# Layer 0's attention joins: statistics stored at an earlier step, merge factors at a later one, two rope turns and the copies of probabilities put at other steps, the last head replanned

## The chip, the cores and the metric

The kernel runs on one core of a Trainium2 chip. The metric is the device time of one execution in microseconds (us); lower is better. A core has five engines that run side by side, each taking its own instructions strictly in order: TensorE (PE in the profile; its weight loads are shown as PEld), VectorE (DVE), ScalarE (ACT), GpSimd (POOL) and SyncE (SP). SP computes nothing here; it issues almost all of the DMAs, also in order. Engines wait for each other through semaphores only.

## The reference

A decoder trunk of two layers over 1024 tokens of width 1024. Layer 0 mixes tokens by dilated softmax attention, layer 1 by gated linear attention; a squared-ReLU MLP follows each. The change touches layer 0's attention only:

```python
DILATED_GROUPS = ((128, 1), (512, 4), (2048, 16))
def dilated_attention(h, w_in, w_out):
    qkv = (h @ w_in).reshape(B, S, N_GROUPS, 3, ATTN_HEADS, HEAD_DIM)
    for g, (window, dil) in enumerate(DILATED_GROUPS):
        q = apply_rope(qkv[:, :, g, 0], cos, sin) * (HEAD_DIM ** -0.5)
        k = apply_rope(qkv[:, :, g, 1], cos, sin)
        v = qkv[:, :, g, 2]
        o_g, lse_g = dilated_group_attention(q, k, v, dil, window // dil)
    alpha = softmax(stack(lses), axis=0)
    o = sum(alpha[..., None] * stack(outs))
    return o.reshape(B, S, ATTN_WIDTH) @ w_out
```

There are 8 heads of 128 channels and, per head, three groups with dilations 1, 4 and 16. Each group has its own queries, keys and values. A query row's three softmax results are weighted by their denominators (the "merge factors") and added.

## The kernel before

All large products are split into three matmuls of float32 halves (high and low parts) and use a seven-product scheme for 2 by 2 blocks. Values of all heads are computed first and kept in DRAM (`vscr`). Then the 24 **passes** p = 3h + g of `Heads` run, one per head h and group g. A pass computes one group's queries and keys of one head with 14 half products (7 slots of `SLOTS`, two halves each, six matmuls of 128x512 per half), and after each half `advance()` moves a counter, the **clock**, one step on. So pass p covers clocks c = 14p to c + 14, and everything else is hung between the half products by the clock: `at(t, fn, rank)` puts a function on clock t, and functions of one clock are issued in order of rank (5 if not given). This order is the program order of every engine's queue.

What hangs on the clock of a pass that starts at c:

- `keep` (ACT, line 1475, rank 0): copies of the product banks ("e1" at c+3, "e5" at c+7, "e2" at c+9, "e3" at c+13). "e5" must be out before the slot that starts after clock c+8 adds to the same bank V again; "e2" before the slot that starts after c+10 adds to X.
- `column` (DVE, line 1438, rank 1) at c+5, c+11, c+13 and c+15: makes half a query or key block; SP then copies its two partition halves crosswise (`cw`, lines 1439 and 1440). The function `turn` inside it (DVE, lines 1447 to 1455, rank 6) applies the rope with that copy, four clocks later.
- `load` (SP, line 1430) at c+3 fetches the next pass's weights in four DMAs of 256 KB, and `stage` cuts them into halves (ACT line 791, DVE lines 792 to 829).
- `follow` hangs the previous pass's attention on this one: `scores` (PE), `soft` (DVE and ACT: bias, minimum, exponential with sums; the numbers kept are the group's statistics), and `send`, which stores the statistics in DRAM (SP). For the first two groups this is `Attention`, for the third `Classes`. Each has scores at c+8 on; `Classes` has all its scores at c+8.
- `Join` merges head h-1 during the passes of head h; its clocks count from c = 14 * 3h. `begin` (SP, lines 1344 to 1348) loads the statistics of all three groups, `factors` (DVE and one ACT, lines 1358 to 1364) makes the merge factors, `spread` scales the stored probabilities by them (the third group on DVE, line 1311, the others block by block on ACT, line 1239), `turn` and `turn_classes` transpose probabilities on PE (lines 1262, 1318), `values` and `values_classes` copy the transposes out of PSUM on ACT (lines 1398, 1385) and multiply with the values on PE (lines 1271, 1326), `keep_classes` copies the third group's result (ACT, line 1392), and `join` adds (DVE, line 1405).

Seven heads are joined in this way. The eighth is joined in `tail`, during the output projection `out_proj`: there each block of 12 matmuls (`tick`) moves the clock two steps on. `W.pump` at the end of a tick loads and cuts projection weights (SP line 133, ACT line 152, DVE line 153); from the seventh block of the first half of the projection on it may run ahead by four loads. `drain_to` runs the rest of the clock up to the first half of the last join, and the second half of the projection goes on with the clock.

Tiles come from pools of fixed numbers of buffers (`t2`: 8 of 2 KB per partition, `k4`: 25 of 4 KB), banks of PSUM from a pool of 8.

Of the kernel before, what the change touches and what calls it, by code (L numbers as in the profile page):

```python
# [9 lines left out]
F32 = mybir.dt.float32  # L10
# [3 lines left out]
AF = mybir.ActivationFunctionType  # L14
# [5 lines left out]
P = 128  # L20
# [4 lines left out]
HEADS = 8  # L25
# [16 lines left out]
def hybrid_trunk(ctx, tc, x, norm_mix, norm_mlp, norm_fin, a_in, a_out, g_in, g_up, g_b, g_nw,  # L42
# [16 lines left out]
    def t2(shape, dt, name):  # L59
        return wk.tile(shape, dt, name=name, tag="t2", bufs=8)  # L60
# [14 lines left out]
    steps = deque()  # L75
# [186 lines left out]
    class Split:  # L262
# [4 lines left out]
        @staticmethod  # L267
        def at(tiles, k):
            n = 4 // len(tiles)
            return tiles[k // n][:, k % n, :]  # L270
# [489 lines left out]
    class Up:  # L760
# [96 lines left out]
        def copy(self, p, name):  # L857
            e = t2([P, 512], F32, name)
            act.activation(e, self.st[p]["X"], AF.Copy)  # L859
            self.st[p][name] = e  # L860
# [293 lines left out]
    clock = [0]  # L1154
# [36 lines left out]
    class Attention:  # L1191
# [74 lines left out]
        def values(self, half, po, t):  # L1266
            at_ = 0
            for i, (k, c, where) in enumerate(self.pieces(half)):
                n = 128 * len(c)
                o = po[:, where:where + n] if self.g == 0 else po.rearrange("p (m r) -> p r m", r=4)[:, where, :]  # L1270
                pe.matmul(o, self.v[:, k, :], t[:, at_:at_ + n], start=self.g == 0 and i == 0, stop=True,  # L1271
                          skip_group_check=True)
                at_ += n
# [5 lines left out]
            at(c + send, self.send)  # L1279

    class Classes(Attention):
        SOFT = 9, 10, 11, 12
        SEND = 13

        def scores(self, j):
            if j:
# [45 lines left out]
    class Join:  # L1332
# [48 lines left out]
            self.ps = self.g[2].turn()  # L1381

        def values_classes(self):
            t = t2([P, 512], F32, "pt")
            act.activation(t, self.ps, AF.Copy)
            self.po = self.g[2].values(t)

        def keep_classes(self):
            self.k = k4([P, S], F32, "oc")
# [1 line left out]
            for q in range(2):  # L1391
                act.activation(to[:, q], self.po[q].rearrange("p (i e m) -> p i e m", i=4, e=2), AF.Copy)

        def values(self, g, half):
            banks = self.banks.pop((g, half))
            t = (t2 if len(banks) == 1 else k4)([P, 512 * len(banks)], F32, "pt")
            for i, (ps, n) in enumerate(banks):
                act.activation(t[:, 512 * i:512 * i + n], ps[:, :n], AF.Copy)
            if g == 0:
                self.sum = bank("pO")  # L1400
            self.g[g].values(half, self.sum, t)
# [10 lines left out]
    class Heads(Up):  # L1412
# [20 lines left out]
        def column(self, p, b, half, bank_, e):  # L1433

            h, g = divmod(p, NG)
            c = t2([P, 512], F32, "c")
            w = t2([P, 512], F32, "cw")
            dve.tensor_tensor(c, bank_, e, op=OP.add)  # L1438
            sp.dma_start(w[0:64, :], c[64:128, :])
            sp.dma_start(w[64:128, :], c[0:64, :])  # L1440

            def turn():
                sl = slice(512 * half, 512 * half + 512)
                if (p, b) not in self.dst:
                    self.dst[p, b] = k4([P, S], F32, ("qT", "kT")[b])
                dst = self.dst[p, b]
                dve.tensor_tensor(w, w, ctab[:, 1, sl], op=OP.mult)  # L1447
                dve.tensor_tensor(c, c, ctab[:, 0, sl], op=OP.mult)
                if g == 0:
                    dve.tensor_tensor(dst[:, sl], c, w, op=OP.add)  # L1450
                else:
                    r = 4 if g == 1 else 16
                    n = 512 // r
                    o = dst.rearrange("p (r m) -> p r m", r=r)[:, :, n * half:n * half + n]
                    dve.tensor_tensor(o, c.rearrange("p (m r) -> p r m", r=r),
                                       w.rearrange("p (m r) -> p r m", r=r), op=OP.add)
            at(clock[0] + (3 if p == self.count - 1 and half else 4), turn, 6)

        def remain(self, fn):
            if self.behind:  # L1460
# [6 lines left out]
        def plan(self, p):  # L1467
            c = 14 * p
            st = self.st.setdefault(p, {})
            self.behind = True  # L1470

            def keep(b, name):
                def fn():
                    e = t2([P, 512], F32, name)
                    act.activation(e, st[b], AF.Copy)  # L1475
                    st[name] = e
                return fn
            at(c + 3, keep("X", "e1"), 0)
            at(c + 5, lambda: self.column(p, 0, 0, st["Y"], st["e1"]), 1)
            at(c + 7, keep("V", "e5"), 0)  # L1480
            at(c + 9, keep("X", "e2"), 0)
            at(c + 11, lambda: self.column(p, 1, 0, st["V"], st["e2"]), 1)
            at(c + 13, keep("X", "e3"), 0)
            at(c + 13, lambda: self.column(p, 1, 1, st["X"], st["e5"]), 1)
            at(c + 15, lambda: self.column(p, 0, 1, st["Z"], st["e3"]), 1)
            if p == 0:
                for s, t in ((4, 1), (6, 3), (5, 5)):
                    at(c + t, lambda s=s: self.stage(p, s), 7)
            at(c + 3, lambda: self.load(p + 1))
            for s, t in ((0, 8), (1, 9), (2, 10), (3, 11), (4, 14), (6, 15), (5, 17)):  # L1490
                at(c + t, lambda s=s: self.stage(p + 1, s), 1.5 if s in (1, 3, 6) else 7)

# [46 lines left out]
        keep_head(h, half, o)  # L1539
        reached.add((0, half))  # L1540

    def join_steps(load, first, gap=1):

        n = lambda k: first + int(gap * k)
        return ((load, 5, "begin"),
                (n(0), 9, "factors"), (n(0), 9.1, "spread", 2, None),
                (n(1), 5, "load_values", 2), (n(1), 9, "spread", 0, range(4)), (n(3), 5, "load_values", 0),
                (n(3), 9, "spread", 0, range(4, 8)), (n(4), 5, "load_values", 1),
                (n(4), 3, "turn_classes"), (n(4), 9, "spread", 1, range(0, 8, 2)),
                (n(5), 4, "values_classes"), (n(5), 9, "spread", 1, range(1, 8, 2)),  # L1550
                (n(6), 0.5, "keep_classes"), (n(6), 3, "turn", 0, 0),
                (n(7), 0.6, "values", 0, 0), (n(7), 3, "turn", 1, 0),
                (n(8), 0.6, "values", 1, 0), (n(8), 3, "turn", 0, 1),
                (n(9), 0.6, "values", 0, 1), (n(9), 0.5, "join", 0), (n(9), 3, "turn", 1, 1),
                (n(10), 0.6, "values", 1, 1),
                (n(11), 0.6, "join", 1))


    vals = RawValues(a_in, [(3 * g + 2) * AW for g in range(NG)], lambda g: vscr[:, g, :])
# [235 lines left out]
    for p in range(heads.count):  # L1795
        h, g = divmod(p, NG)
        if g == 0 and h:
            Join(h - 1, joined).plan(14 * p, join_steps(15, 19))
        if p == heads.count - 1:
            for k in range(0, KT, 2):  # L1800
                add_rows(a_out, k)
            c = 14 * p
            at(c + 1, lambda: turned.load(0), 0)
            at(c + 3, lambda: (W.dma(), W.dma()), 0)
            at(c + 4, lambda: (W.dma(), W.dma()), 0)
            for t in (7,8,9,10):
                at(c + t, lambda: W.prep(dve), 7)
            at(c + 8, lambda: turned.turn(0), 7)
            at(c + 9, lambda: (turned.load_x(0), turned.load_x(1)))
            at(c + 11, lambda: turned.turn(1), 7)  # L1810
        heads.run_head(p)

    def drain_to(mark):
        while mark not in reached:
            steps.popleft()()
            now[0] += 1
            run_due()

    def tail():

        c = clock[0]
        heads.follow(heads.count - 1, c, (7, 7, 8, 8), (8, 8, 9, 9), 10)
        turned.load(1)
        Join(HEADS - 1, last_joined).plan(c, join_steps(13, 18, 1.5))
        rows = {}

        def early(half):
            t = rows[half] = h8([P, 4, 512], F32, "ol2")
            sp.dma_start(t[:, 0:3, :], oscr[4:7, :, 512 * half:512 * half + 512].rearrange("h p c -> p h c"))

        def turn(half, h):
            keep_head(h, half, rows[half][:, h - 4, :])

        def weights():
            W.early = RAW
        at(c + 1, lambda: early(0))
        at(c + 28, weights)
        at(c + 20, lambda: early(1))
        for t, half, h in ((10, 0, 4), (12, 0, 5), (14, 0, 6), (29, 1, 4), (31, 1, 5), (33, 1, 6)):
            at(c + t, lambda half=half, h=h: turn(half, h))  # L1840
        steps.extend([advance] * 44)

    tail()

# [1 line left out]
    def out_proj(layer, wbc_row, o, up):  # L1846
# [55 lines left out]
        for tb in range(NB):  # L1902
            if tb == 2:
                drain_to((layer, 1))
            for n in range(2):
                if n:
                    st.middle(tb)
                add_block(tb, lambda k: tuple(t[:, k % 2, 128 * (tb % 4):128 * (tb % 4) + 128]
                                              for t in oT1[tb // 4, k // 2]), w, n)
            st.after(tb)  # L1910
# [728 lines left out]
```

## Time and profile before

| | |
|---|---|
| median of 3 runs | 2634.8 us (2633.99 to 2635.62) |
| the profiled execution | 2633.89 us |
| its span, first to last instruction | 2631.6 us |
| PE busy | 2577.8 us, 98% |
| DVE busy | 1856.8 us, 71% |
| ACT busy | 1271.7 us, 48% |
| the 24 passes | about 244 to 896 us of the span |
| one head (three passes) | 82.45 us |

A row of the view of instructions in order of time has the start, the duration, the engine, the line, the operation, and in brackets how long the engine had been idle and what ended that. "PE L854" are the pass's matmuls. SPq rows are DMA issues. A row of the view of waits has who waited for whom: microseconds in total, times, longest. PEclk in the view of stretches is the granted clock of PE, 1.00 being full speed.

### The profile page before, as it was taken

What the parts mean: (1) busy time and instruction counts of PE and PEld (TensorE: products, weight loads), DVE (VectorE), ACT (ScalarE), POOL (GpSimd) and SP (SyncE); (2) the same over time, 40 slices, a digit from 0 to 9 for tenths busy, and PEclk for the clock granted to TensorE, in tenths of its full rate; (3) what the DMA queues carried; (4) which work ended last, traced back from release to release, by engine and by line L of the source; (5) the groups of instructions that cost most, each with busy time, mean ns of one, the idle gap of its engine ahead of it and who ended that gap; (6) DMA issues with size and microseconds to landing.
All of it is one profiled execution on the core that took longest, in us unless ns stands there. A gap on an engine that the chain in (4) does not pass through costs nothing.

```text
span 2631.6 us, 33955 instructions
## 1 busy us (share of the span) xinstructions
PE 2577.8 (98%) x12391; PEld 2133.9 (81%) x12391; DVE 1856.8 (71%) x2926; ACT 1271.7 (48%) x2243; POOL 17.9 (1%) x26
## 2 busy tenths in 40 slices
PE   9999999999999899999999999999999999999999
PEld 7888877778777778888888888888888888888887
DVE  8766977787777646687767787687676566656567
ACT  7443444545545335566554454554335455553344
POOL 0000000000000000000000000010000000000000
PEclk9999999999999999999999999999999999999999
DMA  5785445444445555789888966777545745396544
GB/s 187 251 292 164 101 106 110 105 98 98 106 104 112 149 149 204 248 299 321 307 323 302 312 218 214 251 246 262 212 156 183 269 137 172 116 339 213 188 146 134
DMA packets 367511, 519.96 MB, mean 198 GB/s; under 512 B 73216, under 2 KB 188688, under 8 KB 367344
## 3 DMA queue, kind: packets, MB, share of 16 engines
q1 hardware_dynamic: 367040, 517.40, 61.2%
q8 instruction: 97, 1.59, 0.2%
q14 instruction: 70, 0.57, 0.1%
q10 hardware_dynamic: 304, 0.40, 0.0%
HBM read 327.20 MB, written 165.35 MB: 187 GB/s over the span
## 4 chain that ended last, share of the span: by engine, by line
PE 81%; DVE 7%; DMA 5%; ACT 3%; issue 2%; SPq 1%; DVEq 0%; ACTq 0%
PE pB L1991 13%; PE pX L854 13%; PE pA L1991 10%; PE pV L854 9%; PE pB L1066 8%; PE pA L1066 6%; PE pZ L854 5%; PE pY L854 4%; DMA cw<-c 3%; PE pd L196 2%; PE pd L198 2%; PE pd L197 2%; PE pO L1271 2%; DVE c L1438 1%; DMA stats<-st 1%
## 5 line engine op out<-in xcount | busy, mean ns | idle before, releaser
L1991 PE MATMUL pB<-dh 128*128 128x512 f32 x512 | 199.2, 389 | 0.0
L1991 PE MATMUL pB<-dl,dh 128*128 128x512 f32 x512 | 199.2, 389 | 0.0
L1991 PE MATMUL pB<-dh,dl 128*128 128x512 f32 x512 | 199.2, 389 | 0.0
L854 PE MATMUL pV<-s4h,wd 128*128 128x512 f32 x480 | 171.0, 417 | 25.3 <-ACT e L1475 25.3
L205 DVE TENSOR_TENSOR dl<-sin,dh 128x1024 fp32r<-128x1024 f32 x112 | 136.6, 1220 | 63.3 <-ACT dh L202 60.7
L202 ACT ACTIVATE dh<-sin 128x1024 fp32r<-128x1024 f32 x112 | 117.8, 1052 | 77.9 <-PE pB L1991 29.9
L1991 PE MATMUL pA<-dh 128*128 128x512 f32 x384 | 149.6, 390 | 0.0
L1991 PE MATMUL pA<-dh,dl 128*128 128x512 f32 x384 | 149.4, 389 | 0.0
L1991 PE MATMUL pA<-dl,dh 128*128 128x512 f32 x384 | 149.4, 389 | 0.0
L859 ACT ACTIVATE e<-pX 128x512 f32<-128x512 f32 x108 | 64.5, 597 | 158.6 <-PE pX L854 158.5
L202 ACT ACTIVATE dh<-kept 128x1024 fp32r<-128x1024 f32 x64 | 67.8, 1060 | 146.6 <-DVE kept L1956 102.7
L854 PEld LDWEIGHTS pV<-s4h,wd 128*128 128x128 f32 x480 | 95.1, 198 | 48.5 <-ACT e L1475 28.1
L1991 PEld LDWEIGHTS pB<-dl,dh 128*128 128x128 f32 x512 | 96.1, 188 | 20.1
L1991 PEld LDWEIGHTS pB<-dh 128*128 128x128 f32 x512 | 96.1, 188 | 19.9
L1991 PEld LDWEIGHTS pB<-dh,dl 128*128 128x128 f32 x512 | 96.1, 188 | 19.8
L792 DVE TENSOR_TENSOR wbl<-t,wbh 128x1024 fp32r<-128x1024 f32 x48 | 58.7, 1224 | 62.3 <-ACT wbh L791 62.3
L854 PE MATMUL pX<-s3h,wgh 128*128 128x512 f32 x240 | 96.6, 402 | 2.3 <-ACT e L1475 2.3
L854 PE MATMUL pV<-s4l,wd 128*128 128x512 f32 x240 | 97.8, 407 | 0.0
L1447 DVE TENSOR_TENSOR cw<-cw,tab 128x512 f32<-128x512 f32 x96 | 65.9, 687 | 44.5 <-DMA cw<-c 44.3
L854 PE MATMUL pZ<-a22h,wgh 128*128 128x512 f32 x240 | 96.5, 402 | 0.0
L854 PE MATMUL pX<-a11h,wah 128*128 128x512 f32 x240 | 96.5, 402 | 0.0
L854 PE MATMUL pY<-a12h,wah 128*128 128x512 f32 x240 | 93.8, 391 | 0.0
(381 smaller groups left out, 7185.6 us busy)
## 6 DMA issues: line engine op xcount, KB each, us to landing
sin<-acts SPq DMA_DIRECT2D x112, 512.0 KB, 4.7
acts<-s SPq DMA_DIRECT2D x64, 512.0 KB, 3.5
raw<-in_mlp_w_down_dram SPq DMA_DIRECT2D x64, 512.0 KB, 5.2
raw<-in_attn_w_in_dram SPq DMA_DIRECT2D x96, 256.0 KB, 5.6
cw<-c SPq DMA_DIRECT2D x192, 128.0 KB, 2.4
raw<-in_mlp_w_up_dram SPq DMA_DIRECT2D x48, 512.0 KB, 6.0
acts<-c SPq DMA_DIRECT2D x64, 256.0 KB, 2.8
kept<-in_mlp_w_down_dram SPq DMA_DIRECT2D x32, 512.0 KB, 7.1
```

Source lines behind the costliest of these rows:

```text
L196: pe.matmul(ps, sh, mh, start=start, stop=False)
L197: pe.matmul(ps, sh, ml, start=False, stop=False)
L198: pe.matmul(ps, sl, mh, start=False, stop=stop)
L202: act.activation(hi, src, AF.Copy)
L205: dve.tensor_tensor(lo, src, hi.bitcast(F32), op=OP.subtract)
L792: self.remain(lambda: dve.tensor_tensor(lo, src, hi.bitcast(F32), op=OP.subtract))
L854: pe.matmul(st[b], u[:, k, :], v, start=first and k + n == 0, stop=k == 3 and n == 2, skip_group_check=True)
L859: act.activation(e, self.st[p]["X"], AF.Copy)
L1066: pe.matmul(self.acc[s][t], parts[k][v == 2][:, 128 * t:128 * t + 128], (th, tl)[v == 1][:, k, :], start=fresh and m + k + v == 0, stop=m ...
L1271: pe.matmul(o, self.v[:, k, :], t[:, at_:at_ + n], start=self.g == 0 and i == 0, stop=True, skip_group_check=True)
L1447: dve.tensor_tensor(w, w, ctab[:, 1, sl], op=OP.mult)
L1991: pe.matmul(self.acc[s][t], a[:, k, c], b[:, k, :], start=fresh and m + k + v == 0, stop=m == 7 and k == 1 and v == 2, skip_group_check=True)
```

## The change

Durations and amounts of work stay the same; functions move to other clocks and ranks.

- `Classes.SOFT` goes from 9, 10, 11, 12 to 9, 9, 9, 10 and `SEND` from 13 to 11: the third group's softmax and the store of its statistics.
- `values` and `values_classes` are split into a `copy` (ACT) and the matmuls; in a clock all copies now go ahead of the matmuls (ranks 0.6 and 0.65; `copy_classes` 0.6 and `values_classes` 4).
- In passes of the first group (g = 0) the rope turn of the second half of the queries goes from clock c+19 to c+20, that of the keys from c+17 to c+21.
- `join_steps` is written anew, with one table for the seven heads (`HEAD`) and one for the last (`LAST`). `begin` stays at 15 for the seven; `factors` goes from 19 to 21; the third group's `spread` from 19 to 23, its `turn_classes` from 23 to 25, its values from 24 to 26 and `keep_classes` from 25 to 28; the first group's `spread` from four blocks each at 20 and 22 to two at 21, four at 22 and two at 23; the second group's from four each at 23 and 24 to four each at 26 and 28; value loads of the third, first and second group from 20, 22, 23 to 20, 22, 22; the first transposes of the other groups from 25 to 26, and the two joins from 28 and 30 to 29 and 31.
- The last head: softmax from 8, 8, 9, 9 to 9, 9, 10, 10, store from 10 to 11, `begin` from 13 to 15, `factors` from 18 to 19, `turn_classes` from 24 to 26, and the other steps with it; the second half's rows of earlier heads are split at 33, 35, 37 instead of 29, 31, 33. More `advance` steps are laid out and the remaining ones dropped at the third row block of the second half.
- `load` in `Heads.plan` gets the rank 5 written out, which it had.

```diff
     class Classes(Attention):
-        SOFT = 9, 10, 11, 12
-        SEND = 13
+        SOFT = 9, 9, 9, 10
+        SEND = 11
...
         def values_classes(self):
-            t = t2([P, 512], F32, "pt")
-            act.activation(t, self.ps, AF.Copy)
-            self.po = self.g[2].values(t)
+            self.po = self.g[2].values(self.t)
+
+        def copy_classes(self):
+            self.t = t2([P, 512], F32, "pt")
+            act.activation(self.t, self.ps, AF.Copy)
...
-        def values(self, g, half):
+        def copy(self, g, half):
             banks = self.banks.pop((g, half))
             t = (t2 if len(banks) == 1 else k4)([P, 512 * len(banks)], F32, "pt")
             for i, (ps, n) in enumerate(banks):
                 act.activation(t[:, 512 * i:512 * i + n], ps[:, :n], AF.Copy)
+            self.banks[g, half] = t
+
+        def values(self, g, half):
+            t = self.banks.pop((g, half))
...
-            at(clock[0] + (3 if p == self.count - 1 and half else 4), turn, 6)
+            wait = 3 if p == self.count - 1 and half else 4
+            if g == 0 and half:
+                wait = (5, 8)[b]
+            at(clock[0] + wait, turn, 6)
...
-    def join_steps(load, first, gap=1):
+    HEAD = dict(s2=2, v2=-1, v1=1, sp0=(0, 1, 1, 2), t2=4, o2=5)
+    LAST = dict(s2=1, v2=1, v1=4, sp0=(1, 1, 3, 3), t2=5, o2=6)
+
+    def join_steps(load, first, w, gap=1):
 
         n = lambda k: first + int(gap * k)
-        return ((load, 5, "begin"),
-                (n(0), 9, "factors"), (n(0), 9.1, "spread", 2, None),
-                (n(1), 5, "load_values", 2), (n(1), 9, "spread", 0, range(4)), (n(3), 5, "load_values", 0),
-                (n(3), 9, "spread", 0, range(4, 8)), (n(4), 5, "load_values", 1),
-                (n(4), 3, "turn_classes"), (n(4), 9, "spread", 1, range(0, 8, 2)),
-                (n(5), 4, "values_classes"), (n(5), 9, "spread", 1, range(1, 8, 2)),
-                (n(6), 0.5, "keep_classes"), (n(6), 3, "turn", 0, 0),
...
+        t = 5
+        pairs = ((0, 2), (4, 6), (1, 3), (5, 7))
+        steps = [(load, 5, "begin"), (n(0), 9, "factors"), (n(w['s2']), 9.1, "spread", 2, None)]
+        steps += [(n(w['v2']), 4, "load_values", 2), (n(1), 5, "load_values", 0), (n(w['v1']), 5, "load_values", 1)]
+        steps += [(n(w['sp0'][i]), 9, "spread", 0, range(2 * i, 2 * i + 2)) for i in range(4)]
+        steps += [(n((5, 5, 7, 7)[i]), 9, "spread", 1, pairs[i]) for i in range(4)]
+        steps += [(n(w['t2']), 3, "turn_classes"), (n(w['o2']), 0.6, "copy_classes"),
+                  (n(w['o2']), 4, "values_classes"), (n(7), 0.5, "keep_classes")]
+        order = ((0, 0), (1, 0), (0, 1), (1, 1))
+        for i, (g, half) in enumerate(order):
+            steps += [(n(t + i), 3, "turn", g, half), (n(t + i + 1), 0.6, "copy", g, half),
+                      (n(t + i + 1), 0.65, "values", g, half)]
+        return steps + [(n(t + 3), 0.5, "join", 0), (n(t + 5), 0.6, "join", 1)]
...
-            Join(h - 1, joined).plan(14 * p, join_steps(15, 19))
+            Join(h - 1, joined).plan(14 * p, join_steps(15, 21, HEAD))
...
-        heads.follow(heads.count - 1, c, (7, 7, 8, 8), (8, 8, 9, 9), 10)
+        heads.follow(heads.count - 1, c, (7, 7, 8, 8), (9, 9, 10, 10), 11)
         turned.load(1)
-        Join(HEADS - 1, last_joined).plan(c, join_steps(13, 18, 1.5))
+        Join(HEADS - 1, last_joined).plan(c, join_steps(15, 19, LAST, 1.5))
...
-        for t, half, h in ((10, 0, 4), (12, 0, 5), (14, 0, 6), (29, 1, 4), (31, 1, 5), (33, 1, 6)):
+        for t, half, h in ((10, 0, 4), (12, 0, 5), (14, 0, 6), (33, 1, 4), (35, 1, 5), (37, 1, 6)):
             at(c + t, lambda half=half, h=h: turn(half, h))
-        steps.extend([advance] * 44)
+        steps.extend([advance] * 60)
...
                 drain_to((layer, 1))
+                if not layer:
+                    steps.clear()
```

More of the change, by code (lines that the diff above doesn't have):

```diff
@@ L1488, in plan @@
                     at(c + t, lambda s=s: self.stage(p, s), 7)
-            at(c + 3, lambda: self.load(p + 1))
+            at(c + 3, lambda: self.load(p + 1), 5)
             for s, t in ((0, 8), (1, 9), (2, 10), (3, 11), (4, 14), (6, 15), (5, 17)):
@@ L1540, in last_joined @@
         reached.add((0, half))
-    def join_steps(load, first, gap=1):
+    HEAD = dict(s2=2, v2=-1, v1=1, sp0=(0, 1, 1, 2), t2=4, o2=5)
+    LAST = dict(s2=1, v2=1, v1=4, sp0=(1, 1, 3, 3), t2=5, o2=6)
+    def join_steps(load, first, w, gap=1):
         n = lambda k: first + int(gap * k)
-        return ((load, 5, "begin"),
-                (n(0), 9, "factors"), (n(0), 9.1, "spread", 2, None),
-                (n(1), 5, "load_values", 2), (n(1), 9, "spread", 0, range(4)), (n(3), 5, "load_values", 0),
-                (n(3), 9, "spread", 0, range(4, 8)), (n(4), 5, "load_values", 1),
-                (n(4), 3, "turn_classes"), (n(4), 9, "spread", 1, range(0, 8, 2)),
-                (n(5), 4, "values_classes"), (n(5), 9, "spread", 1, range(1, 8, 2)),
-                (n(6), 0.5, "keep_classes"), (n(6), 3, "turn", 0, 0),
[L1552 to L1556, printed above, removed]
+        t = 5
[11 more added lines that the diff above has]
+        return steps + [(n(t + 3), 0.5, "join", 0), (n(t + 5), 0.6, "join", 1)]
     vals = RawValues(a_in, [(3 * g + 2) * AW for g in range(NG)], lambda g: vscr[:, g, :])
```

## The prediction, made before the changed kernel had run

> **What bounds the kernel now.** PE works nearly all of the span, so I first read what PE waits for, over the whole span, and take only what the moved steps can reach.
>
> ```profile
> span 2631.6 us, 33955 instructions
> ```
>
> ```profile
> PE pV L854 <- ACT e L1475: 25.3, 7, 4.2
> PE pO L1271 <- ACT pt L1398: 6.1, 9, 1.4
> PE pS L1292 <- DVE qT L1455: 4.7, 4, 3.4
> PE pP L1318 <- DVE pr L1311: 3.1, 1, 3.1
> ```
>
> Seven waits, one per joined head, hold 25.3 us: PE wants to add to bank V again and ACT has not yet copied it out ("e5"). The 6.1 us fall on nine copies of transposes, the 3.1 us on the last head's third group. PE idles little elsewhere, so no edit here can save more than these waits and what follows from them.
>
> What follows is a slow clock. The view of stretches, over the 8 us after each of the seven waits (first and last row of seven):
>
> ```profile
> 342.10:350.10 8.00, 7.92 (x52) 6.46 (x52) 4.43 (x7) 7.24 (x20) 0.00 (x0) 0.80 1.07 210
> ...
> 841.10:849.10 8.00, 7.95 (x36) 6.36 (x38) 5.99 (x11) 7.23 (x20) 0.00 (x0) 0.62 0.98 207
> ```
>
> PEclk is the third number from the right. The seven read 0.80, 0.62, 0.79, 0.81, 0.79, 0.79, 0.62, so 1.6 + 3.0 + 1.7 + 1.5 + 1.7 + 1.7 + 3.0 = 14.2 us are lost there while PE counts as busy. One such wait costs 25.3/7 = 3.6 us plus 2.0 us.
>
> Then the second of the seven in order of time, engine by engine: PE, ACT, DVE, SP.
>
> ```profile
> 420.42 0.81 PE L1203 MATMUL pS<-kT,qT 128*128 128x128 f32 x4
> 424.67 0.80 PE L854 MATMUL pV<-s4h,wd 128*128 128x512 f32 x1 [3.44 <-ACT e L1475]
> ```
>
> ```profile
> 422.54 1.60 ACT L1239 ACTIVATE pr<-pr,stat 128x128 f32<-128x128 f32 x4 [1.17 <-DVE stat L1364]
> 424.04 0.58 ACT L1475 ACTIVATE e<-pV 128x512 f32<-128x512 f32 x1
> ```
>
> ```profile
> 410.05 0.69 DVE L1438 TENSOR_TENSOR c<-pX,e 128x512 f32<-128x512 f32 x1 [0.42 <-ACT e L1475]
> ...
> 420.58 0.22 DVE L1358 TENSOR_REDUCE mz<-stat 128x24 f32<-128x72 f32 x1
> ...
> 427.61 0.69 DVE L1447 TENSOR_TENSOR cw<-cw,tab 128x512 f32<-128x512 f32 x1 [3.82 <-DMA cw<-c]
> ...
> 429.96 0.70 DVE L792 TENSOR_TENSOR wal<-raw,wah 128x512 fp32r<-128x512 f32 x1
> ...
> 433.45 0.42 DVE L1225 CUSTOM_DVE_ANT_0 pr<-pS,masks 128x256 f32<-128x256 f32 x1
> ```
>
> ```profile
> 408.46 0.60 SPq L1440 DMA_DIRECT2D cw<-c  x1
> ...
> 411.97 1.27 SPq L1308 DMA_DIRECT2D stats<-st  x2
> ...
> 415.75 0.37 SPq L1344 DMA_DIRECT2D stat<-stats  x1
> ...
> 418.28 2.27 SPq L1430 DMA_DIRECT2D raw<-in_attn_w_in_dram  x4
> ```
>
> PE is ready for bank V at 420.42 + 0.81 = 421.2. ACT copies it at 424.04 because four `spread` blocks stand ahead in its queue, and they wait for `factors`, which DVE runs from 420.58 to 422.5. DVE shows no idle time before 420.58: the statistics were there, DVE was behind. So storing them sooner is by itself worth nothing at this point. What frees PE is the order on ACT: "e5" at clock 21 (rank 0) now stands ahead of `factors` (rank 9) and of every `spread`.
>
> **The change part by part, for this head.** No instruction is added or taken away.
>
> *The 3.4 us wait and its slow clock go.* Bank V is complete before 421.2 and ACT then has nothing late ahead of "e5". The next copy, "e2" at clock 23, has the factors' exponential, six blocks of the first group at 0.4 us (the 1.60 us of four) and one weight cut ahead. Factors: DVE loses the key turn at 17 and does it at 21, ahead of `factors`, so they start about 1 us earlier than now, near 419.5; "e2" is done near 425.0. PE wants it after two half products and one score.
>
> ```profile
> 363.95 0.86 PE pS L1203 x4
> 364.82 0.87 PE pP L1262 x8
> 365.69 1.39 PE pX L854 x6
> ```
>
> A half product is 1.39 us, a score pair 0.86, eight transposes 0.87. So PE wants "e2" at 421.2 + 2 x 1.39 + 0.86 = 424.9: level, at worst some tenths.
>
> *A new wait comes.* The third group's `spread` now stands at clock 23 with rank 9.1, behind the turn of that clock (rank 6), and DVE waits for that turn's `cw` copy: today 3.82 us, until 427.61. Behind it on DVE wait the turn, a weight cut, the spread and all that follows; PE waits for the spread with `turn_classes` (clock 25), and ACT's `copy_classes` (clock 26) stands behind the first group's second softmax (clock 25), which DVE reaches last. When does that copy land? It follows the four weight loads in SP's queue. Here they start at 418.28 and the copy lands 9.3 us later; the extremes of the seven heads are
>
> ```profile
> 585.26 2.27 SPq L1430 DMA_DIRECT2D raw<-in_attn_w_in_dram  x4
> ```
>
> ```profile
> 595.58 0.69 DVE L1447 TENSOR_TENSOR cw<-cw,tab 128x512 f32<-128x512 f32 x1 [4.99 <-DMA cw<-c]
> ```
>
> and
>
> ```profile
> 835.06 2.27 SPq L1430 DMA_DIRECT2D raw<-in_attn_w_in_dram  x4
> ```
>
> ```profile
> 843.04 0.69 DVE L1447 TENSOR_TENSOR cw<-cw,tab 128x512 f32<-128x512 f32 x1 [2.78 <-DMA cw<-c]
> ```
>
> 10.3 us and 8.0 us (four of the seven are near 8.0). SP gets to these loads earlier now. Four third-group blocks no longer stand ahead of "e3" on ACT and of the column at 410.05 on DVE, which gains about 1 us (0.42 idle, four blocks of softmax). The store goes out right behind the copy pair that ends at 409.06, not after 411.97; from its issue to the first statistics load pass 415.75 - 411.97 = 3.8 us, so these loads go at 412.9, just after the two later copy pairs, and the weights at 415.4 instead of 418.28. **That 2.9 us is what the earlier store buys.** The copy lands at 415.4 + 8.0 to 10.3, so 423.4 to 425.7, that is 2.2 to 4.5 us after PE is ready at 421.2.
>
> From landing to the end of that softmax DVE takes 433.87 - 427.61 = 6.3 us today, with the spread 6.9; an exponential and the PSUM copy on ACT add about 1.1. PE reaches `values_classes` after four half products (5.56), two score pairs (1.72) and eleven transposes (1.2), 8.5 us after 421.2. So PE loses (landing + 8.0) - 8.5, **1.7 to 4.0 us per head**. Its larger part (turn 2.35 from 427.61 to 429.96, cut and spread 0.6 each: landing + 3.6 against 5.0) stands before the transposes, the rest before the values, so mostly no single gap is as long as today's. I take 2.5 us without slow clock: most heads are near 8.0, three near 10. Seven heads: 17.5 us.
>
> The Trainium skill ("DMA: Bandwidth & Descriptors", "Queues, rings and completion order") says that a DMA engine takes descriptors of one ring in order; by that the later value loads could not hold up the copy and every head would land at 8.0, which makes 12 us instead of 17.5. The 10.3 us above speaks against it.
>
> *Copies ahead of values:* the 6.1 us hold seven waits of 0.5 to 0.7 us in the heads. Copies and transposes are now a clock apart with `keep_classes` in between on ACT; I count half of some 4.5 us as saved, bounds 0 and 4.5, or a loss of as much if ACT's queue fills.
>
> *Edits at nothing:* the query turn at 20 and the key turn at 21 are done before the scores of clock 22 and wanted in full at 26; PE work hides them, and if DVE were 2 us later there, the scores would wait. The rank 5 was the default. The earlier third-group softmax fills DVE's wait for a copy at clock 9. The later row splits in the tail are wanted only in the second half's fifth row block. More buffers are held at once, `t2` up to its 8 by my count at clock 19; the ones taken there are free by then.
>
> *The last head.* Now SP sits on the statistics before it sends the projection weights, DVE waits for those, and the factors stand behind:
>
> ```profile
> 923.50 0.38 SPq L1344 DMA_DIRECT2D stat<-stats  x1
> ...
> 926.82 2.04 SPq L133 DMA_DIRECT2D raw<-in_attn_w_out_dram  x4
> ```
>
> ```profile
> 932.16 2.54 DVE L153 TENSOR_TENSOR wlo<-raw,whi 128x1024 fp32r<-128x1024 f32 x2 [8.93 <-ACT whi L152]
> ```
>
> With `begin` at 15 the weights go first, at about 922; the cuts end near 930, factors run near 931 to 934, and `turn_classes` comes one block later, near 938. The 3.1 us wait goes, with a slow clock of about 1.7 (like the shorter of the seven): 4.8 us, bounds 0 and 6. The other tail waits (3.4 of the 4.7 us) stand before the moved steps and stay.
>
> **Sum:** 25.3 + 14.2 + 2.2 + 4.8 - 17.5 = 29.0 us. The profiled execution took 2633.89 us (2.3 around its span), 0.9 below the median: 2633.9 - 29 = 2605.
>
> The Trainium skill ("TensorE: Matmul & The Clock Gate", "What's actually happening") says that PE falls to half rate after an idle window of about 3.4 us and returns after a busy one. By it seven throttles are worth 7 x 1.7 = 12 us (an estimate from that page), the sum 27. The rows say 14.2 and decide.
>
> **Rivals.**
> - *Nothing takes the wait's place:* the copy lands some 2 us sooner than computed, because the loads meet an emptier DMA. For it: DVE has 3.8 us of idle time there today. Against: four heads show the same 8.0. Then 25.3 + 14.2 + 4.5 + 4.8 = 49 saved: 2585.
> - *The new wait nearly eats the old one:* landing near 10.3 everywhere, 4.0 per head and no gain on copies: 28 + 0 against 44: some 12 to 17 saved, 2617 to 2622.
> - *Nothing measurable:* the same, with the slow clock in some heads: within 5 us of 2634.
> - *Slower:* SP gets no lead. If the weight loads start no earlier against PE than at 418.28, the copy lands at 427.61, PE stands 427.6 + 8.0 - 421.2 - 8.5 = 5.9 us per head, 5.0 of it in one piece before `turn_classes`, long enough for the slow clock of 2.0: 7 x 7.9 = 55 against 25.3 + 14.2 + 4.8 = 44: 2645. It decides from a lead under about 1 us. For it: SP is in order and DVE is full up to that point. Against: the store's own wait is visible and moves.
> - *The change does not do what it says:* "e5" is still late, because ACT waits for something else: 2634. Nothing in the rows shows that.
>
> **How the numbers follow.** A measurement of this kernel can tell about 0.2%, 5 us, from no change. Forecast (2596 to 2614) 0.54; nothing in its place (2583 to 2592) 0.18; nearly eaten (to 2625) 0.14; nothing measurable 0.06; slower 0.08. The range 2584 to 2623 holds the first, nearly all of the second and most of the third.
>
> **What would show it.** Right: no wait of pV on "e" in the passes; a new wait of PE on line 1318 or 1326 of 1 to 3 us per head; weight loads on SP about 3 us earlier against the scores of clock 22; PEclk near 1.00 there. Wrong: waits of over 3.4 us with PEclk at half; `cw` landing less than 7 or more than 11 us after the first weight load; pP on DVE in the tail still there.

## The result, and the profile after

The changed kernel takes 2605.1 us (median of 4 runs, 2603.54 to 2605.39) against 2634.4 us for the kernel before in 4 runs (2631.57 to 2635.62): ratio 0.9889, 95% interval 0.9872 to 0.9906. The profiled span went from 2631.6 to 2603.3 us, by 28.3. PE's busy time went from 2577.8 to 2565.1 us, though both profiles count the same 12391 matmuls: these 12.7 us of the gain I put down to a slow clock that is gone. The other 15.6 us are idle time of PE (53.8 before, 38.2 after).

In the lines below "e" is copied at line 1484 (1475 before), a `turn` starts at 1453 (1447), weight loads are issued at 1436 (1430) and `copy_classes` stands at 1388 (1385). First the waits of PE over the whole span of the changed kernel: who waited for whom, total us, times, longest.

```profile
PE pP L1318 <- DVE pr L1311: 12.3, 7, 3.0
PE pX L854 <- ACT e L1484: 5.4, 7, 1.8
PE pS L1292 <- DVE qT L1461: 4.2, 2, 3.8
PE pO L1326 <- ACT pt L1388: 4.0, 5, 0.8
...
PE pO L1271 <- ACT pt L1400: 1.1, 1, 1.1
```

The row "pV on e" with its 25.3 us is gone. Three rows took its place: transposes of the third group on the spread (12.3, one wait per head), bank X on "e2" (5.4, one per head), values of the third group on the copy of the transposes (4.0, in five heads). That is 21.7 us, but cut into pieces of 0.3 to 3.0.

The second head again, in order of time: PE, ACT, DVE and SP of the changed kernel.

```profile
417.00 0.81 PE L1203 MATMUL pS<-kT,qT 128*128 128x128 f32 x4
...
421.69 0.50 PE L854 MATMUL pX<-s3h,wgh 128*128 128x512 f32 x1 [0.26 <-ACT e L1484]
...
424.86 0.66 PE L1318 MATMUL pP<-ident,pr 128*128 128x128 f32 x4 [1.50 <-DVE pr L1311]
...
429.33 2.07 PE L1326 MATMUL pO<-pt,v 64*128 64x64 f32 x32 [0.80 <-ACT pt L1388]
```

```profile
414.53 0.60 ACT L1484 ACTIVATE e<-pV 128x512 f32<-128x512 f32 x1 [3.90 <-PE pV L854]
```

```profile
416.27 0.22 DVE L1358 TENSOR_REDUCE mz<-stat 128x24 f32<-128x72 f32 x1
...
421.18 0.69 DVE L1453 TENSOR_TENSOR cw<-cw,tab 128x512 f32<-128x512 f32 x1 [2.43 <-DMA cw<-c]
...
424.13 0.67 DVE L1311 TENSOR_TENSOR pr<-pr,stat 128x512 f32<-128x512 f32 x1
```

```profile
409.59 0.45 SPq L1344 DMA_DIRECT2D stat<-stats  x1
...
412.31 2.21 SPq L1436 DMA_DIRECT2D raw<-in_attn_w_in_dram  x4
414.62 0.49 SPq L1445 DMA_DIRECT2D cw<-c  x1
```

ACT now waits for PE's bank V (3.90 idle) instead of PE for ACT. Read the four queues from the bottom up: the `cw` copy is issued behind four weight loads, lands 421.18 - 412.31 = 8.9 us after the first of them, DVE stands 2.43 us for it, then turns, then spreads at 424.13, and PE's transposes had waited 1.50 us by 424.86. The weight loads go out 417.00 - 412.31 = 4.7 us ahead of the scores; before it was 420.42 - 418.28 = 2.1. The lead over the scores grew by 2.6 us in this head. In the seven heads it grew by 2.8, 2.6, 1.8, 1.4, 2.1, 3.2 and 1.9 us, by 2.2 on average.

The clock, in the view of stretches (PEclk third from the right): the new waits' stretch of the second head, and those of the third and fourth.

```profile
420.00:430.00 10.00, 7.44 (x45) 5.63 (x45) 7.91 (x14) 7.19 (x20) 0.00 (x0) 1.00 0.79 162
```

```profile
504.00:514.00 10.00, 7.05 (x54) 6.01 (x53) 8.13 (x16) 5.71 (x15) 0.00 (x0) 0.83 0.43 99
588.00:598.00 10.00, 8.89 (x61) 7.62 (x62) 6.75 (x16) 6.79 (x18) 0.00 (x0) 0.83 0.40 93
```

Five heads keep 1.00 (the other four read as the second does); the third and fourth lose 1.7 us each, 3.4 together where there were 14.2.

### The profile page after: what moved, and what is told of

It is laid out like the page before. It is cut to its first block, busy times and chain, and to the rows that moved or that the text cites. A ratio compares the mean times of both kernels' runs of the same rounds, so it can differ in the third digit from the quotient of the medians.

```text
span 2603.3 us, 33979 instructions
## 1 busy us (share of the span) xinstructions
PE 2565.1 (99%) x12391; PEld 2125.5 (82%) x12391; DVE 1853.8 (71%) x2926; ACT 1273.1 (49%) x2243; POOL 17.9 (1%) x26
## 4 chain that ended last, share of the span: by engine, by line
PE 86%; DVE 5%; DMA 4%; issue 2%; ACT 1%; SPq 1%; DVEq 0%; ACTq 0%
PE pX L854 15%; PE pB L2006 13%; PE pA L2006 10%; PE pV L854 10%; PE pB L1066 8%; PE pA L1066 6%; PE pZ L854 5%; PE pY L854 5%; DMA cw<-c 3%; PE pd L196 2%; PE pd L198 2%; PE pd L197 2%; PE pO L1271 2%; DVE c L1444 1%; PE pS L1203 1%
## 5 line engine op out<-in xcount | busy, mean ns | idle before, releaser
L854 PE MATMUL pV<-s4h,wd 128*128 128x512 f32 x480 | 161.3, 398 | 0.0
L854 PE MATMUL pX<-s3h,wgl 128*128 128x512 f32 x240 | 94.5, 394 | 0.0
L854 PE MATMUL pX<-s3l,wgh 128*128 128x512 f32 x240 | 94.4, 393 | 0.0
L854 PE MATMUL pX<-a11h,wal 128*128 128x512 f32 x240 | 93.6, 390 | 0.0
```

The source lines that it names most:

```text
L854: pe.matmul(st[b], u[:, k, :], v, start=first and k + n == 0, stop=k == 3 and n == 2, skip_group_check=True)
```

## The experiments

My theory: the gain is the wait on "e5" with its slow clock; what is left is one chain, SP's weight loads, then the `cw` copy, DVE's turn, the spread, and PE. By it the store matters only through SP's lead, the turns do not matter, and anything that takes the spread or the copy of the transposes away from that copy gains more. The rivals: the order on ACT is all there is to it, and the store is idle; or the gain lies in the turns or in the tail. Each ratio is to runs of the kernel before on the same chip; the chips differ by some us, so rows are compared by their ratios.

| kernel | median us | ratio | 95% interval |
|---|---|---|---|
| the change | 2605.1 | 0.9889 | 0.9872 to 0.9906 |
| before, first spreads one clock later | 2642.8 | 1.0041 | 1.0026 to 1.0056 |
| before, store sooner | 2623.1 | 0.9966 | 0.9955 to 0.9977 |
| before, new steps of seven heads | 2629.5 | 0.9994 | 0.9985 to 1.0004 |
| before, new last head | 2623.0 | 0.9979 | 0.9969 to 0.9989 |
| change, old store | 2623.4 | 0.9968 | 0.9956 to 0.9980 |
| change, old turns | 2603.5 | 0.9894 | 0.9878 to 0.9911 |
| change, third group's spread at 21 | 2595.3 | 0.9878 | 0.9864 to 0.9891 |
| the same, transposes 24 and their copy 25 | 2584.8 | 0.9834 | 0.9821 to 0.9848 |
| change, weight loads behind the copy | 2580.0 | 0.9814 | 0.9800 to 0.9827 |
| before, weight loads behind the copy | 2630.5 | 1.0001 | 0.9991 to 1.0011 |
| change, both of the gaining edits | 2576.8 | 0.9797 | 0.9782 to 0.9811 |

### Only the order on ACT, in the kernel before

```diff
-                (n(1), 9, "spread", 0, range(4))
+                (n(2) if gap == 1 else n(1), 9, "spread", 0, range(4))
```

> The kernel before with one step moved: the first four spread blocks of the first group go from clock 20 to 21, so that ACT reaches the copy e5 (rank 0 of clock 21) ahead of them. Theory (order on ACT): the seven waits of pV on e (25.3 us) shrink to under 1 us each and the slow clock behind them (14.2 us) goes; e2 at clock 23 then stands behind eight spread blocks and one weight cut and gives back some 1.3 us per head. About 25 us faster than before, near 2609. Rival (the late factors themselves bound PE): the wait only moves to pX on e2 with the same 3.4 us and slow clock, and the time stays within 5 us of before.

This missed: the kernel got slower by 0.4%, 11 us. The waits of PE, then ACT and PE of the second head:

```profile
PE pO L1326 <- ACT pt L1385: 25.1, 7, 3.6
PE pV L854 <- ACT e L1475: 6.2, 7, 1.5
```

```profile
422.96 0.58 ACT L1475 ACTIVATE e<-pV 128x512 f32<-128x512 f32 x1
424.22 1.60 ACT L1239 ACTIVATE pr<-pr,stat 128x128 f32<-128x128 f32 x4 [0.69 <-DVE stat L1364]
...
429.72 1.26 ACT L1239 ACTIVATE pr<-pr,stat 128x128 f32<-128x128 f32 x4
430.89 0.58 ACT L1385 ACTIVATE pt<-pP 128x512 f32<-128x512 f32 x1
```

```profile
431.52 4.03 PE L1326 MATMUL pO<-pt,v 64*128 64x64 f32 x32 [3.58 <-ACT pt L1385]
```

The wait on "e5" fell from 25.3 to 6.2 us, as meant, and 25.1 us came up at the next thing that hangs on the same engine: the copy of the transposes stands behind twelve of the sixteen spread blocks, as it did before, and PE, no longer held at "e5", is now there ahead of it (ACT works without a gap from 424.2 to 431.5). One long wait per head at another place, a slow clock again (0.988 over the run, 0.992 before), and nothing won. The order on ACT removes the old wait but does not by itself make the gain: the change also spaces the blocks out and moves transposes and values two clocks later.

### The store alone, and the change without it

In the first, `SOFT = 9, 9, 9, 10` and `SEND = 11` are put into the kernel before; in the second the old numbers into the changed one:

```diff
-        SOFT = 9, 9, 9, 10
-        SEND = 11
+        SOFT = 9, 10, 11, 12
+        SEND = 13
```

> The kernel before with only the third group's softmax at 9, 9, 9, 10 and its store at 11. Theory (DVE is behind, the statistics are not late): factors start at most 1 us earlier, the waits of pV on e stay at 2.5 us or more per head with the slow clock, 0 to 8 us faster than before. Rival (the store is what PE waits for): the weight loads on SP and the factors come 3 us earlier, the waits go, 25 us or more faster.

> The changed kernel with the third group's softmax back at 9, 10, 11, 12 and its store back at 13. Theory (the earlier store buys SP a lead of 2.5 to 2.9 us for the weight loads and the cw copy behind them, and PE now waits for that copy through the third group's spread): PE waits 2 to 2.9 us more per head on lines 1318 and 1326, 14 to 20 us slower than the changed kernel, near 2622, more if a wait passes 3.4 us and the clock drops. Rival (the store's place is of no use): within 4 us of the changed kernel, 2601 to 2609.

Alone the store gives 0.34%, some 9 us, just above what I had allowed, and in four heads the wait falls under the 2.5 us that I had set. Of the kernel before with the new store: the waits, then PE and DVE of the second head.

```profile
PE pV L854 <- ACT e L1475: 19.5, 7, 4.1
```

```profile
420.68 0.82 PE L1203 MATMUL pS<-kT,qT 128*128 128x128 f32 x4
...
423.67 0.50 PE L854 MATMUL pV<-s4h,wd 128*128 128x512 f32 x1 [2.17 <-ACT e L1475]
```

```profile
409.06 0.68 DVE L1438 TENSOR_TENSOR c<-pX,e 128x512 f32<-128x512 f32 x1
...
419.58 0.22 DVE L1358 TENSOR_REDUCE mz<-stat 128x24 f32<-128x72 f32 x1
```

The same wait, 2.17 us here instead of 3.44. The column that stood at 410.05 with 0.42 us of idle time runs at 409.06 without, and DVE is early from there on: the factors start 1.1 us ahead of the scores (420.68 - 419.58), where before they started 0.2 behind them (420.42 and 420.58). Those 1.3 us are what the wait lost. It is so in every head: against the scores the factors move by 1.1, 1.3, 1.2, 0.1, 1.1, 1.4 and -0.3 us, and each wait shrinks by as much (in the last one it grows). Taken out of the change, the store costs 0.8%, some 20 us (ratio 0.9968 against 0.9889). The waits and SP's loads of the changed kernel with the old store:

```profile
PE pP L1318 <- DVE pr L1311: 21.9, 7, 4.1
PE pX L854 <- ACT e L1484: 11.6, 7, 3.7
```

```profile
418.73 2.27 SPq L1436 DMA_DIRECT2D raw<-in_attn_w_in_dram  x4
```

```profile
420.95 0.82 PE L1203 MATMUL pS<-kT,qT 128*128 128x128 f32 x4
```

The loads are back to 2.2 us ahead of the scores, and two of the new waits nearly double (12.3 to 21.9, 5.4 to 11.6), while the third falls from 4.0 to 0.7. The time came out about as expected, but not its parts. On lines 1318 and 1326 together PE waits 0.9 us more per head, not 2 to 2.9; "e2" adds another 0.9, and PE's busy time is 6.2 us longer. The row of "e2" goes by the factors and not by the copy: with either store its wait is, in all seven heads, the start of the factors minus the start of the scores plus 0.99 us (here 420.67 - 420.95 + 0.99 = 0.71). So, against my theory, the store brings two things in the new order, SP's lead and earlier factors; no run separates what each is worth.

### The new steps of the seven heads alone

The kernel before with only `HEAD`'s steps; store, turns and last head as before (the last head keeps the old list of steps).

```diff
-            Join(h - 1, joined).plan(14 * p, join_steps(15, 19))
+            Join(h - 1, joined).plan(14 * p, join_steps(15, 21, HEAD))
```

> The changed kernel's join steps for the seven heads alone: third group's softmax and store, rope turns and the last head as before. Theory (without SP's lead the copy lands as late as before, and the plan trades the wait on e5 for one on the spread of the same size): PE waits 20 us or more on lines 1318 and 854, ratio 0.996 to 1.001. Rival (the plan is what saves, the store adds): ratio 0.990 to 0.994.

```profile
PE pP L1318 <- DVE pr L1311: 27.6, 8, 4.7
PE pX L854 <- ACT e L1484: 9.6, 7, 3.0
```

No difference can be measured (0.9994). These are its waits of PE: the 25.3 us are gone and 27.6 + 9.6 stand there instead (one of the eight in the last head). The steps alone are worth 0.06%, the store alone 0.34%, the last head 0.21%, the turns nothing: together 0.6%. The whole is 1.1%. Without the store the parts do add up (0.32% for the change with the old store, 0.06 + 0.21 alone); the store is worth 0.34% in the old order and some 0.8% in the new one, where the copy and the factors that it brings forward are what PE waits for.

### The turns, and the last head

The changed kernel with the old turns, and the kernel before with the new last head only (`LAST`, `begin` at 15, softmax 9, 9, 10, 10, store 11, rows at 33, 35, 37, more steps).

```diff
-                wait = (5, 8)[b]
+                wait = 4
```

> The changed kernel with the two rope turns of first-group passes back at clocks 17 and 19. Theory (DVE does the same work ahead of the factors either way, and SP issues the cw copy behind the weight loads, later than DVE needs it): within 4 us of the changed kernel, 2601 to 2609. Rival (the moved turns free DVE for the column ahead of them by 1.9 us, and this reaches PE): 1 to 1.9 us per head, 7 to 13 us slower, 2612 to 2618.

> The kernel before with only the last head's join, softmax, store and row splits as in the change. Theory: the wait of pP on the spread in the tail (3.1 us) and the slow clock behind it go, 3 to 6 us faster than before. Rival (the projection weights or the stored statistics bind there whatever the order): within 1.5 us of before.

The turns make no difference (0.9894 against 0.9889). The last head gives 0.21%, 5.5 us, interval 2.9 to 8.1. Its wait for the third group's spread (3.1 us) is not among the waits of that kernel any more, while the passes are as they were:

```profile
PE pV L854 <- ACT e L1484: 25.8, 7, 5.5
```

### Cutting the new chain: spread and copies sooner

First the third group's spread back by two clocks, ahead of the turn that waits for the copy; then also transposes and their copy a clock sooner each:

```diff
-    HEAD = dict(s2=2, v2=-1, v1=1, sp0=(0, 1, 1, 2), t2=4, o2=5)
+    HEAD = dict(s2=0, v2=-1, v1=1, sp0=(0, 1, 1, 2), t2=4, o2=5)
```

```diff
-    HEAD = dict(s2=2, v2=-1, v1=1, sp0=(0, 1, 1, 2), t2=4, o2=5)
+    HEAD = dict(s2=0, v2=-1, v1=1, sp0=(0, 1, 1, 2), t2=3, c2=4, o2=5)
...
-(n(w['o2']), 0.6, "copy_classes"),
+(n(w['c2']), 0.6, "copy_classes"),
```

> The changed kernel with only the third group's spread put back right behind the factors (clock 21, rank 9.1), out of the reach of the cw wait. Theory (two waits in a row hang on the copy's landing: the spread, and behind it on ACT the copy of the transposes, queued after the second softmax): the 12.3 us of pP on the spread shrink to under 2 us, and pO L1326 on the copy rises from 4.0 to about 11 us; only the 0.6 us of the spread leave the chain, so 3 to 6 us faster than the changed kernel, 2599 to 2602. Rival (the spread's wait is the whole): 12 us faster, about 2593.

> The same, and the third group's transposes at clock 24 instead of 25 and their copy at clock 25, rank 0.6, ahead of the second softmax on ACT. Theory: both waits on lines 1318 and 1326 go (16 us together with the spread's), and about 0.9 us per head come back at the first group's copy of transposes, which stands behind the same softmax: 8 to 12 us faster than the changed kernel, 2593 to 2597. Rival (ACT's whole pile is what is late, as with the spread moved alone): the wait moves on in full, within 4 us of the changed kernel.

The waits of the first, then of the second:

```profile
PE pO L1326 <- ACT pt L1388: 12.7, 7, 3.0
PE pX L854 <- ACT e L1484: 4.3, 7, 1.3
```

```profile
PE pO L1271 <- ACT pt L1400: 5.6, 10, 1.1
...
PE pX L854 <- ACT e L1484: 1.3, 3, 0.6
```

With the spread out of the chain, the same wait comes up one step later, at the values (4.0 to 12.7 us), and the ratio moves from 0.9889 to 0.9878 only, which the intervals don't tell apart. With the copy of the transposes also ahead of the late softmax, the wait is gone, and the kernel is 0.55% (14 us) faster than the change, somewhat more than expected.

### Cutting it at its source: the weight loads behind the copy

In the passes of the second group (the join's clock 17) the loads of the next weights go two clocks later, to 19, behind the `cw` pair in SP's queue; the same in the kernel before; then in the changed kernel together with the last edit.

```diff
-            at(c + 3, lambda: self.load(p + 1), 5)
+            at(c + (5 if p % NG == 1 else 3), lambda: self.load(p + 1), 5)
```

> The changed kernel with the weight loads of second-group passes at clock c+5 (rank 5, behind the column of rank 1 and its cw copy) instead of c+3. Theory (the cw copy lands late because it queues behind 1 MB of weights): it lands some 3 us after its issue, DVE no longer waits there, the waits on lines 1318 and 1326 (16 us) go; the weights come about 1.5 us later and cost up to 1 us per head at the cut ahead of e2: 8 to 16 us faster than the changed kernel, 2589 to 2597. Rival (DVE or ACT is late by itself, or the later weights bind as much): within 4 us of the changed kernel or slower.

> The kernel before with only the weight loads of second-group passes behind the column's cw copy (clock c+5). Theory (in the order before, PE hangs on the factors' and spreads' place on DVE and ACT, not on that copy; only the changed order made the copy the bound): the seven waits of pV on e stay near 25 us with their slow clock, within 5 us of before, ratio 0.998 to 1.002. Rival (an earlier copy is worth the same in either order): 15 us or more faster, ratio under 0.994.

> The weight loads behind the copy, and also the third group's spread at clock 21, its transposes at 24 and their copy at 25. Theory: with the copy early the two moves find no wait left on lines 1318 and 1326, so they add nothing, and the spread at 21 may take 0.6 us of DVE ahead of the first softmax: ratio 0.980 to 0.983, like the loads alone (0.9814). Rival (the two remove different waits and add up, 14 and 20 us): ratio near 0.976.

SP, DVE and the waits of PE in the changed kernel with this one number:

```profile
410.83 0.49 SPq L1445 DMA_DIRECT2D cw<-c  x1
411.37 0.60 SPq L1446 DMA_DIRECT2D cw<-c  x1
412.06 2.22 SPq L1436 DMA_DIRECT2D raw<-in_attn_w_in_dram  x4
```

```profile
416.97 0.69 DVE L1453 TENSOR_TENSOR cw<-cw,tab 128x512 f32<-128x512 f32 x1
```

```profile
PE pX L854 <- ACT e L1484: 3.9, 7, 1.2
PE pS L1292 <- DVE qT L1461: 3.2, 1, 3.2
PE pO L1271 <- ACT pt L1400: 1.5, 2, 1.1
```

The copies go out ahead of the loads, DVE's turn carries no bracket, so it did not wait, and two of the three new rows (12.3 and 4.0 us) are gone. 0.9814: another 0.75%, some 20 us, on top of the change, a little more than the 8 to 16 expected. In the kernel before the same edit is worth nothing (1.0001), since the copy was not on its path: PE waited there for "e5".

```profile
PE pV L854 <- ACT e L1475: 23.7, 7, 4.7
```

Both edits together give 0.9797, the fastest kernel here and just under the 0.980 to 0.983 expected: 2576.8 us, 2.0% below before. Their gains don't add up (0.55 and 0.75 give 0.92), as two cuts of one chain wouldn't; that the second still adds something to the first is not beyond the intervals.

## Why the prediction was right, and where not

Predicted 2605, measured 2605.1. That the sum came out this well is luck: errors of both signs met. By its own terms:

| term | predicted us | measured us | from |
|---|---|---|---|
| wait on "e5" | 25.3 | 25.3 | the row is gone |
| its slow clock | 14.2 | 10.8 | 3.4 stay, in two heads |
| copies ahead of values | 2.2 | 5.0 | 6.1 to 1.1 us |
| last head | 4.8 | 5.5 (2.9 to 8.1) | last head alone |
| new waits | -17.5 | -21.7 | 12.3 + 5.4 + 4.0 |
| sum | 29.0 | 24.9 | span: 28.3 |

- **The wait and its cause: right.** "e5" now runs the moment PE is done with bank V, and ACT waits for PE.
- **The slow clock: too large a term.** I took it as gone with the long waits. In the third head a wait of 2.95 us and in the fourth one of 2.10 were still followed by half the clock.
- **The new wait and its mechanism: right, its size somewhat small.** It goes through the `cw` copy, the turn, the spread, and then the copy for the values, as laid out. For the second head the sum with a landing after 9.3 us gave 3.0; the copy landed after 8.9 and the three waits are 0.26 + 1.50 + 0.80 = 2.6. Over the seven heads 2.5 us per head became 3.1.
- **The landing: right on average.** It took 8.1, 8.9, 9.8, 9.2, 8.0, 8.8 and 9.1 us, with a mean of 8.8, and 8.8 is also the mean of the seven before. Only "four heads near 8.0, three near 10" was no property of the heads.
- **SP's lead: nearly right in the second head (2.9 predicted, 2.6 measured), too large on average.** Its mean gain over the seven is 2.2 us. The 0.7 us that are missing per head make 4.7 in seven, about the 4.2 between 17.5 and 21.7. This agrees in size only: the sum's own formula, with each head's landing and lead, gives 25.4.
- **"e2" level with PE: in four heads.** There it waits 0.3 us; in the other three it waits 1.2 to 1.8, because the factors, expected 0.9 us ahead of the scores, start 0.2 to 0.8 behind them. I counted nothing for it. Its 5.4 us are inside the 21.7; the two waits that I did count come to 16.3. As a wait on "e2" holds PE back ahead of the next one, the three are one chain, and I compare their total.
- **"Storing sooner is by itself worth nothing at this point": wrong.** It gives 9 us in the old order. I asked only whether the statistics were there in time (they were). The microsecond that DVE gains at the column, which I did count for SP's lead, moves the factors too, and with them the old wait.
- **"What frees PE is the order on ACT": only half of it.** With that order alone the wait reappears at the copy of the transposes and the kernel is slower. The lead of SP belongs to the gain too (the change with the old store shows it); whether the later transposes and values do was not tested singly; the part-by-part costs held for the whole and not for its pieces.
- **Turns at nothing: right. Copies: the direction right, half the size,** with a part of it coming back as the 4.0 us of the third group's copy.
- **The rivals.** "Nothing takes its place" is near to what the kernel with the loads behind the copy shows: 0.9814 of 2634.4 is 2585, the time worked out, though 3.9 us of waits on "e2" stay. The "slower" rival asked for a lead under 1 us; with the old store the lead was all but lost, and that kernel still gained 0.3%, 0.2% of it from the last head: its waits of 5.9 us per head were priced too high. They come to 21.9 + 11.6 = 33.5 us, 4.8 per head.

The terms leave 3.4 us of the span's 28.3 unexplained. A part is a single wait of the kernel before in its last pass, which is no longer there; why was not traced.

```profile
PE pX L854 <- ACT e L1475: 2.3, 1, 2.3
```

## What to carry to other kernels

In queues that run in order, a wait that is taken away can come up at the next instruction that hangs on something late, as it did here in three kernels. So a plan is priced by what is late next, and its parts need not be worth in sum what they are worth together. Find the late source: here it was a pair of 128 KB copies queued behind 1 MB of weights, and putting them ahead, one number, gave 0.75% in the new order and nothing in the old one. A long wait cut into pieces also mostly saved the slow clock behind it here: of 14.2 us in seven heads 3.4 stayed, in two.

## What the runs showed of the hardware

The length of one wait alone does not say whether the clock falls. In the fourth head of the changed kernel, by stretches of 1 us:

```profile
587.00:588.00 1.00, 0.01 (x1) 0.00 (x0) 1.00 (x2) 0.51 (x2) 0.00 (x0) 1.00 1.23 246
588.00:589.00 1.00, 0.00 (x0) 0.00 (x0) 1.00 (x3) 0.00 (x0) 0.00 (x0) 1.00 1.14 269
589.00:590.00 1.00, 0.89 (x5) 0.89 (x6) 0.97 (x3) 0.00 (x0) 0.00 (x0) 0.66 0.57 148
590.00:591.00 1.00, 1.00 (x4) 0.81 (x3) 1.00 (x3) 0.58 (x1) 0.00 (x0) 0.50 0.17 46
```

```profile
585.36 0.50 PE L854 MATMUL pX<-s3h,wgh 128*128 128x512 f32 x1 [1.39 <-ACT e L1484]
...
589.11 0.95 PE L1318 MATMUL pP<-ident,pr 128*128 128x128 f32 x4 [2.10 <-DVE pr L1311]
```

A wait of 2.10 us, 1.7 us of work behind one of 1.39, brought PEclk to 0.50; in the seventh head one of 2.2 us, behind one of 1.2, left it at 1.00. The Trainium skill ("TensorE: Matmul & The Clock Gate", "What's actually happening") says that the clock falls after an idle window of some 3.4 us, and that these windows run freely. No wait of the changed kernel in its heads is that long (the longest is 2.95 us); that it goes by activity in a window that the wait happens to meet would fit both heads, but no run here settles it.
